# Differential attention scores: the high-part products of two maps moved into two 64-row halves of the array

## The chip, the cores and the metric

The kernel runs on one core of a Trainium2 chip. The metric is the device time of one execution in microseconds (us). Three runs of the kernel before are shown; beside them stands the profile of one execution. Names used below: PE is TensorE's matrix multiplication, PEld its weight load, DVE is VectorE, ACT is ScalarE, POOL is GpSimd, SP is the engine that issues most DMAs.

## The reference, cut to what matters

One decoder layer for 1024 tokens of width 1024: a projection `z = rms_norm(x) @ w_in`, then two branches side by side (differential softmax attention with 8 heads, gated linear attention with 4 heads), then an output projection with `w_out`, a norm and the residual. The change touches the attention scores alone:

```python
def diff_attention(q, k, v, lam):      # q, k: (B, S, 8 heads, 2 maps, 64)
    q = q * (DA_HEAD_DIM ** -0.5)
    s = jnp.einsum('bqhmd,bkhmd->bhmqk', qb, k)          # per block of 128 queries
    p = jax.nn.softmax(jnp.where(mask, s, -jnp.inf), axis=-1)
    w = p[:, :, 0] - lam * p[:, :, 1]                    # the two maps' difference
    return jnp.einsum('bhqk,bkhv->bqhv', w, v)
```

Each head has two maps, and the contraction of a score is over 64 numbers.

## The kernel before, in words

All products run in float32r. To keep accuracy, an operand is split in two: a high part (the value copied to float32r) and a low part (what is left), and a product `a*b` is built from products of the parts.

**Scores.** In `take` the projected q and k of a head are split and written to DRAM tiles `qk_d` of the shape [map, part, 64, 1024], part 0 being high and part 1 low. `load_qk` brings half a sequence (512 columns) back: the tile `q` holds, for each map, the high part on partitions 0 to 63 and the low part on 64 to 127; `k` holds the same order; `ks` holds k with the two parts swapped. For each block of 128 queries (`qb`, from 7 down to 0) and each map, `scores` multiplies q with k (high times high plus low times low, in one pass over all 128 rows) and q with ks (the two cross terms, in a second pass), both into one PSUM bank. A causal block of n = (qb+1)*128 keys is cut into parts of at most 512 columns (`parts_of`). There are three score banks, used in rotation (`sc_bank`). As each bank is done, DVE reads it with the mask and a running minimum (the instruction that writes `p`); after a map's last part ACT takes the exponential; after the second map DVE, POOL and DVE combine both maps to the weights. In the last head some narrow blocks are multiplied 512 wide, so that the bank is fully written.

**The work around it.** `merge` interleaves three generators into one program order for PE: `all_scores`, `all_values` (which transposes the weights in `turn`, splits them, and multiplies with v in `weigh`, 34 of merge's time units behind the scores) and `out_early` (the output projection's partial sums, tiles `ypart`). Each generator gives the merge an estimated cost at each yield, and the merge takes the one whose planned time is least. `scores` yields once after each DVE read of a bank, so that other PE work can be placed between the passes of one map and those of the next. PE keeps this program order (`mm` pins it); the other engines' order is planned by the framework. `load_qk` for the next head is called when block 4 of a head has been scored, and its DMAs go to SP's queue; `qk_load` remembers the last of them, behind which the gate and v loads are placed.

Every matrix multiplication of the kernel goes through line 142, so groups of instructions are told apart by their tiles: `sc` are the scores, `wtr` the transposed weights, `po` the weighted values, `ypart` and `yps` the output projection, `gkl_ps` a small projection to 64 output columns early in the kernel.

Of the kernel before, what the change touches and what calls it, by code (L numbers as in the profile page):

```python
# [9 lines left out]
F32R = mybir.dt.float32r  # L10
# [4 lines left out]
P = 128  # L15
# [5 lines left out]
DA_HEADS = 8  # L21
# [4 lines left out]
QA, KA, VA, GA, QB, KB, VB, GB, GKL = 0, 1024, 2048, 3072, 4096, 4608, 5120, 6144, 7168  # L26
# [5 lines left out]
def hymba_kernel(  # L32
# [21 lines left out]
    pe, sp = nc.tensor, nc.sync  # L54
# [22 lines left out]
    def fp(t):  # L77
        return t.bitcast(F32)

    def cols(half):  # L80
        return slice(half * 512, half * 512 + 512)
# [47 lines left out]
    def bank(i, shape, name):  # L129
        return psum.tile(shape, F32, tag=f"b{i}", name=name)  # L130
# [10 lines left out]
    def mm(*a, **k):  # L141
        tc.keep_in_program_order(pe.matmul(*a, **k))  # L142
# [32 lines left out]
    kp = ctx.enter_context(tc.tile_pool(name="kp", bufs=1))  # L175
# [9 lines left out]
    def t_st(name, dt=F32):  # L185
        return t2k("st", 4, name, dt)
# [73 lines left out]
    i = order.index((1, 4))  # L260
# [176 lines left out]
    def take(kind, n, half, unit, c):  # L437

        cs = cols(half)
        if kind in ("QA", "KA"):  # L440
            h = n + unit

            ending = made[0] > len(order) - LEAD
            if ending and order[made[0] - 1][1] == 7:
                raw = ap.tile([P, 2, 512], F32R, tag="raw", name="qk_st", bufs=4)
                hi, lo = raw[:, 0], raw[:, 1]
            else:
                hi, lo = t_st("qk_hi", F32R), c.bitcast(F32R)
            scale = -0.125 if kind == "QA" else 1.0
            act.activation(hi, c, AF.Copy, scale=scale)  # L450
            dve.scalar_tensor_tensor(lo, c, scale, fp(hi), ALU.mult, ALU.subtract)
            d = qk_d["q" if kind == "QA" else "k"][h]
            for t, src in enumerate((hi, lo)):
                for m in range(2):
                    ins = sp.dma_start(d[m, t, :, cs], fp(src)[64 * m : 64 * m + 64])
                    if ending:
                        tc.keep_in_program_order(ins)
        elif kind in ("GA", "GB"):
            g = t_st("g")
            act.activation(g, c, AF.Exp, scale=-1.0)  # L460
            act.activation(g, g, AF.Ln, bias=1.0)
            act.activation(g, g, AF.Exp, scale=-1.0)
            dve.tensor_tensor(c, c, g, ALU.mult)
            d = g_d[n + unit] if kind == "GA" else gg_d[n][unit]
            sp.dma_start(d[:, cs], c)
        elif kind == "QB":
            g = n + unit
            e_q, _ = decs[g]
            qd = t_st("gqd")
            dve.scalar_tensor_tensor(c, c, QSCALE, e_q[:, cs], ALU.mult, ALU.mult)  # L470
            dve.tensor_tensor(
                qd.rearrange("p (n i) -> p n i", i=P),
                c.rearrange("p (n i) -> p n i", i=P),
                dsteps[g][:, half * 4 : half * 4 + 4].unsqueeze(2).to_broadcast([P, 4, P]),
                ALU.mult,
            )
            for t, src in enumerate((c, qd)):
                sp.dma_start(gq_d[g][t, :, cs], src)
        else:
            g = n + unit  # L480
            dve.tensor_tensor(c, c, decs[g][1][:, cs], ALU.mult)
            sp.dma_start(gq_d[g][2, :, cs], c)
# [54 lines left out]
    def step(i):  # L537
# [25 lines left out]
        def done(half, unit, p0, p1):  # L563
            if wide(p):
                return take_values(p, half, unit, p0, p1)
            c = t_c("c")
            dve.tensor_tensor(c, p0, p1, ALU.add)
            take(kind, m, half, unit, c)
# [452 lines left out]

    def load_qk(h, n, half):

        if h % 2 and half == 0 and n != "q":
            t = smps[0].tile([P, 2, 512], F32R, tag=f"{n}0", name=f"{n}0")
        else:
            t = kp.tile([P, 2, 512], F32R, tag=f"{n}{half}", name=f"{n}{half}")
        for m in range(2):
            d = qk_d["q" if n == "q" else "k"][h][m, :, :, cols(half)]
            if n != "ks":  # L1030
                ins = sp.dma_start(fp(t[:, m]), d.rearrange("t p s -> (t p) s"))
            else:
                for i in range(2):
                    ins = sp.dma_start(fp(t[64 * i : 64 * i + 64, m]), d[1 - i])
        qk_load[:] = [ins.ins]
        qk[h, n, half] = t

    qk, smps, qk_load = {}, [], []
# [8 lines left out]
    for n in ("q", "k", "ks"):  # L1047
        load_qk(0, n, 1)
        if n != "q":
            load_qk(0, n, 0)  # L1050
# [87 lines left out]
    def parts_of(n):  # L1138
        return [(0, n)] if n <= 512 else [(0, 512), (512, n)]
# [15 lines left out]
    def sc_bank(name, shape):  # L1155
        n_sc[0] += 1
        return bank(SC[n_sc[0] % 3], shape, name)
# [8 lines left out]
    def scores(h, qb):  # L1166

        n = (qb + 1) * P
        qc = slice(qb % 4 * P, qb % 4 * P + P)
        st = const.tile([P, 6], F32, tag="stt", name="stt", bufs=4)  # L1170
        p0 = pp.tile([P, n], F32, tag=f"p0_{qb}", name="p0", bufs=1 + (qb > 5))
        p1 = smp.tile([P, S], F32, tag="p1", name="p1", bufs=2)
        for m, p in enumerate((p0, p1)):
            q = qk[h, "q", qb // 4][:, m, qc]
            parts = parts_of(n)
            if h == DA_HEADS - 1 and (qb, m) in ((1, 1), (0, 0), (0, 1)):

                parts = [(0, 512)]
            for i, (a, b) in enumerate(parts):
                sc = sc_bank("sc", [P, 512])  # L1180
                for j, name in enumerate(("k", "ks")):
                    for half in range(2):
                        lo, hi = max(a, half * 512), min(b, half * 512 + 512)
                        if lo < hi:
                            mm(
                                sc[:, lo - a : hi - a], q,
                                qk[h, name, half][:, m, lo - half * 512 : hi - half * 512],
                                start=(j == 0), stop=(j == 1),
                            )
                e = min(b, n)  # L1190
                last = i == len(parts) - 1

                behind = tc.issue_after(lowest[0]) if (h, qb) == (0, NT - 2) else nullcontext()
                with behind:
                    ins = dve.tensor_tensor_reduce(
                        p[:, a:e], sc[:, : e - a],
                        maskt[:, NZ + P - (e - a) :] if last else maskt[:, : e - a],
                        1.0, 3e38 if i == 0 else st[:, 4 + m : 5 + m], ALU.add, ALU.min,
                        st[:, m : m + 1] if last else st[:, 4 + m : 5 + m],
                    )  # L1200
                if (h, qb) == (0, NT - 1):
                    lowest[:] = [ins.ins]
                c = 0.08 + (e - a) / 512 * 0.56
                if last:
                    act.activation(
                        p[:, :n], p[:, :n], AF.Exp, bias=st[:, m : m + 1], scale=-1.0,
                        accum_out=st[:, 2 + m : 3 + m],
                    )
                if last and m:
                    dve.reciprocal(st[:, 4:6], st[:, 2:4])  # L1210
                    pool.tensor_scalar(
                        p1[:, :n], p1[:, :n], st[:, 5:6], lam, ALU.mult, ALU.mult
                    )
                    dve.scalar_tensor_tensor(
                        p0[:, :n], p0[:, :n], st[:, 4:5], p1[:, :n], ALU.mult, ALU.subtract
                    )
                    w[h, qb] = p0
                    c += 0.25 + n / 1024 * 1.4
                yield c
# [3 lines left out]
    def all_scores():  # L1223
        for h in range(DA_HEADS):
            for qb in range(NT - 1, -1, -1):
                if qb in (3, 5) and h:
                    yield lambda h=h, half=qb // 4: (h - 1, half) in used
                yield from scores(h, qb)
                if qb == 4 and h + 1 < DA_HEADS:
                    for n in ("q", "k", "ks"):  # L1230
                        load_qk(h + 1, n, 1)
                    for n in ("k", "ks"):
                        load_qk(h + 1, n, 0)
            if h + 1 < DA_HEADS:
                load_qk(h + 1, "q", 0)
        scored.append(True)
        opened.update(dict.fromkeys(SC))
# [444 lines left out]
```

## Time and profile before

| | |
|---|---|
| time, median of 3 runs | 973.4 us (973.16 to 973.76) |
| span of the profiled execution | 971.1 us; its page gives no other time of that execution |
| PE busy in the span | 958.7 us (99%), 4977 matmuls and as many weight loads |
| DVE, ACT, POOL busy in the span | 735.5 us (76%), 604.6 us (62%), 207.9 us (21%) |
| mean granted TensorE clock | 0.999 |
| first to last score matmul | 625.8 to 897.1 us of the span |

How to read it: a row of matmuls names the tiles (out<-in), the rows and columns of the array that it uses (128*128), the moving operand's shape (128x512), and its count. The "busy" of a group counts overlapping time once, and a matmul's duration runs to its modelled end, which lies after the start of the next one. What a matmul costs the stream is therefore read from the distance between starts, in the timeline, whose rows give the start, the duration and how many instructions a row holds.

### The profile page before, as it was taken

What the parts mean: (1) busy time and instruction counts of PE and PEld (TensorE: products, weight loads), DVE (VectorE), ACT (ScalarE), POOL (GpSimd) and SP (SyncE); (2) the same over time, 40 slices, a digit from 0 to 9 for tenths busy, and PEclk for the clock granted to TensorE, in tenths of its full rate; (3) what the DMA queues carried; (4) which work ended last, traced back from release to release, by engine and by line L of the source; (5) the groups of instructions that cost most, each with busy time, mean ns of one, the idle gap of its engine ahead of it and who ended that gap; (6) DMA issues with size and microseconds to landing.
All of it is one profiled execution on the core that took longest, in us unless ns stands there. A gap on an engine that the chain in (4) does not pass through costs nothing.

```text
span 971.1 us, 15096 instructions
## 1 busy us (share of the span) xinstructions
PE 958.7 (99%) x4977; PEld 814.5 (84%) x4977; DVE 735.5 (76%) x1464; ACT 604.6 (62%) x1166; POOL 207.9 (21%) x266
## 2 busy tenths in 40 slices
PE   8999999999999999999999999999999999999997
PEld 7998988888888888888888888878888888888786
DVE  5996698897687686686766576587888888898554
ACT  8752364764667555576665344366786787887773
POOL 4300001212141221231100002121322222443322
PEclk9999999999999999999999999999999999999999
DMA  9433366578568987986754588996656769994777
GB/s 347 163 103 117 101 192 225 170 239 294 199 210 255 300 272 251 302 277 212 259 177 152 163 251 269 401 336 203 221 170 218 241 200 355 334 286 106 152 210 148
DMA packets 151293, 220.39 MB, mean 227 GB/s; under 512 B 15728, under 2 KB 86384, under 8 KB 151120
## 3 DMA queue, kind: packets, MB, share of 16 engines
q1 hardware_dynamic: 137056, 178.70, 56.8%
q0 software_dynamic: 14160, 40.74, 14.5%
q8 instruction: 39, 0.64, 0.3%
q14 instruction: 38, 0.31, 0.1%
HBM read 133.93 MB, written 88.60 MB: 229 GB/s over the span
## 4 chain that ended last, share of the span: by engine, by line
PE 94%; ACT 3%; DVE 1%; issue 1%; DMA 0%; POOL 0%; DVEq 0%; ACTq 0%; POOLq 0%
PE x L142 23%; PE z L142 16%; PE y L142 16%; PE ypart L142 13%; PE sc L142 7%; PE po L142 5%; PE yps L142 4%; PE wtr L145 3%; PE gpo L142 3%; PE kv L142 1%; ACT junk L66 1%; PE gkl_ps L142 1%; PE pa L142 1%; DVE p L66 1%; ACT h_hi L66 0%
## 5 line engine op out<-in xcount | busy, mean ns | idle before, releaser
L66 ACT CAST w<-w_raw 128x512 fp32r<-128x512 f32 (+1 forms) x150 | 98.0, 655 | 92.3 <-PE y L142 46.4
L66 DVE TENSOR_TENSOR w<-w_raw,w 128x512 fp32r<-128x512 f32 (+1 forms) x150 | 109.3, 732 | 48.8 <-ACT w L66 44.6
L66 ACT ACTIVATE p<-p,stt 128x896 f32<-128x896 f32 (+7 forms) x128 | 99.3, 777 | 36.2 <-DVE stt L66 35.2
L66 ACT COPY s<-x 128x512 f32<-128x512 f32 x82 | 47.8, 586 | 88.8 <-PE x L142 88.2
L66 POOL TENSOR_SCALAR p<-p,stt,lam 128x1024 f32<-128x1024 f32 (+3 forms) x64 | 56.2, 879 | 147.7 <-DVE stt L66 143.8
L66 DVE CUSTOM_DVE_ANT_0 p<-sc,maskt 128x512 f32<-128x512 f32 (+3 forms) x128 | 74.3, 585 | 14.2 <-PE sc L142 12.9
L66 POOL DMA_DIRECT2D wo_d<-wo_hi x32 | 17.5, 545 | 313.9 <-ACT wo_hi L66 313.9
L142 PE MATMUL z<-s_hi,w 128*128 128x512 f32 x320 | 80.2, 393 | 0.0
L142 PE MATMUL x<-s_hi,w 128*128 128x512 f32 x320 | 80.1, 392 | 0.0
L142 PE MATMUL y<-h_hi,w 128*128 128x512 f32 x320 | 80.0, 392 | 0.0
L142 PE MATMUL ypart<-wo_hi,m_hi 128*128 128x512 f32 x192 | 79.5, 414 | 0.1
L142 PE MATMUL ypart<-wo_hi,m_lo 128*128 128x512 f32 x192 | 75.5, 393 | 0.0
L142 PE MATMUL ypart<-wo_lo,m_hi 128*128 128x512 f32 x192 | 75.4, 393 | 0.0
L142 PE MATMUL sc<-k,q 128*128 128x512 f32 (+1 forms) x192 | 69.1, 363 | 1.4 <-DVE stt L66 1.3
L142 PEld LDWEIGHTS z<-s_hi,w 128*128 128x128 f32 x320 | 59.7, 188 | 12.3
L142 PEld LDWEIGHTS y<-h_hi,w 128*128 128x128 f32 x320 | 59.7, 188 | 12.3
L142 PEld LDWEIGHTS x<-s_hi,w 128*128 128x128 f32 x320 | 59.7, 188 | 12.3
L66 DVE TENSOR_TENSOR w_raw<-w_raw 128x512 f32<-128x512 f32 (+1 forms) x88 | 66.1, 751 | 1.9 <-DMA w_raw<-in_w_in_dram 0.8
L142 PE MATMUL sc<-ks,q 128*128 128x512 f32 (+1 forms) x192 | 66.0, 347 | 0.0
L66 ACT CAST wt_hi<-wtr 128x512 fp32r<-128x512 f32 (+1 forms) x80 | 42.8, 535 | 25.1 <-PE wtr L145 24.3
L66 DVE TENSOR_TENSOR wt_lo<-wtr,wt_hi 128x512 fp32r<-128x512 f32 (+1 forms) x80 | 50.6, 633 | 8.9 <-ACT wt_hi L66 8.2
L66 DVE TENSOR_TENSOR c<-z,s 128x512 f32<-128x512 f32 x48 | 32.8, 688 | 30.6 <-ACT s L66 20.3
(225 smaller groups left out, 2351.7 us busy)
## 6 DMA issues: line engine op xcount, KB each, us to landing
w_raw<-in_w_in_dram SPq DMA_DIRECT2D x48, 512.0 KB, 4.9
wo_d<-wo_hi POOLq DMA_DIRECT2D x32, 256.0 KB, 3.8
q<-q_d SPq DMA_DIRECT2D x32, 256.0 KB, 4.7
k<-k_d SPq DMA_DIRECT2D x32, 256.0 KB, 5.5
ks<-k_d SPq DMA_DIRECT2D x64, 128.0 KB, 6.0
v<-v_d SPq DMA_DIRECT2D x16, 512.0 KB, 7.0
wo_raw<-in_w_out_dram POOLq DMA_DIRECT2D x31, 256.0 KB, 4.8
wo_d<-gqd POOLq DMA_DIRECT2D x22, 256.0 KB, 4.2
```

Of the source, the lines that this page charges most:

```text
L66: ins = op(*a, **k)
L142: tc.keep_in_program_order(pe.matmul(*a, **k))
L145: tc.keep_in_program_order(pe.transpose(dst, src, ident))
```

## The change

In the DRAM tiles the parts are put in another order, by map: q has [high; low] for map 0 and [low; high] for map 1; k has [low; high] for map 0 and [high; low] for map 1. A full load of k's tile now gives `ks`, with the parts opposite to q's. The tile `k` shrinks to [128, 512]: the high part of map 0 on partitions 0 to 63 and the high part of map 1 on partitions 64 to 127. `scores` takes both maps of a part together: it takes two score banks, issues the two cross passes (128 rows, q with ks), then the two products of the high parts (64 rows each, in rows 0 to 63 and in rows 64 to 127), and then the reads. The product of the two low parts is left out. The count of matmuls stays the same, and the yields to `merge` stay after each bank's read.

```diff
+                    at_t = t ^ m if kind == "QA" else 1 - (t ^ m)
+                    ins = sp.dma_start(d[m, at_t, :, cs], fp(src)[64 * m : 64 * m + 64])
...
+        shape = [P, 512] if n == "k" else [P, 2, 512]
...
-            if n != "ks":
+            if n != "k":
                 ins = sp.dma_start(fp(t[:, m]), d.rearrange("t p s -> (t p) s"))
             else:
-                for i in range(2):
-                    ins = sp.dma_start(fp(t[64 * i : 64 * i + 64, m]), d[1 - i])
+                ins = sp.dma_start(fp(t[64 * m : 64 * m + 64]), d[1 - m])
...
-        for m, p in enumerate((p0, p1)):
-            q = qk[h, "q", qb // 4][:, m, qc]
...
-                sc = sc_bank("sc", [P, 512])
-                for j, name in enumerate(("k", "ks")):
-                    for half in range(2):
...
+        for i, (a, b) in enumerate(parts):
+            half, last, e = a // 512, i == len(parts) - 1, b
+            widths = [b - a] * 2
+            if h == DA_HEADS - 1 and qb < 2:
+
+                widths = [b - a if qb else 512, 512]
+            scs = [sc_bank("sc", [P, 512]) for _ in range(2)]
+            for m, sc in enumerate(scs):
+                mm(
+                    sc[:, : widths[m]], q[:, m, qc], qk[h, "ks", half][:, m, : widths[m]],
+                    start=True, stop=False,
+                )
+            for m, sc in enumerate(scs):
+                rows = slice(64 * m, 64 * m + 64)
+                mm(
+                    sc[:, : widths[m]], q[rows, m, qc], qk[h, "k", half][rows, : widths[m]],
+                    start=False, stop=True,
+                )
+            for m, (p, sc) in enumerate(zip((p0, p1), scs)):
```

More of the change, by code (lines that the diff above doesn't have):

```diff
@@ L454, in take @@
                 for m in range(2):
-                    ins = sp.dma_start(d[m, t, :, cs], fp(src)[64 * m : 64 * m + 64])
+                    at_t = t ^ m if kind == "QA" else 1 - (t ^ m)
+                    ins = sp.dma_start(d[m, at_t, :, cs], fp(src)[64 * m : 64 * m + 64])
                     if ending:
@@ L1022, in load_qk @@
     def load_qk(h, n, half):
+        shape = [P, 512] if n == "k" else [P, 2, 512]
         if h % 2 and half == 0 and n != "q":
-            t = smps[0].tile([P, 2, 512], F32R, tag=f"{n}0", name=f"{n}0")
+            t = smps[0].tile(shape, F32R, tag=f"{n}0", name=f"{n}0")
         else:
-            t = kp.tile([P, 2, 512], F32R, tag=f"{n}{half}", name=f"{n}{half}")
+            t = kp.tile(shape, F32R, tag=f"{n}{half}", name=f"{n}{half}")
         for m in range(2):
             d = qk_d["q" if n == "q" else "k"][h][m, :, :, cols(half)]
-            if n != "ks":
+            if n != "k":
                 ins = sp.dma_start(fp(t[:, m]), d.rearrange("t p s -> (t p) s"))
             else:
-                for i in range(2):
-                    ins = sp.dma_start(fp(t[64 * i : 64 * i + 64, m]), d[1 - i])
+                ins = sp.dma_start(fp(t[64 * m : 64 * m + 64]), d[1 - m])
         qk_load[:] = [ins.ins]
@@ L1172, in scores @@
         p1 = smp.tile([P, S], F32, tag="p1", name="p1", bufs=2)
-        for m, p in enumerate((p0, p1)):
-            q = qk[h, "q", qb // 4][:, m, qc]
[L1175 to L1179, printed above, removed]
-                sc = sc_bank("sc", [P, 512])
-                for j, name in enumerate(("k", "ks")):
-                    for half in range(2):
[L1183 to L1191, printed above, removed]
+        q = qk[h, "q", qb // 4]
+        parts = parts_of(n)
+        for i, (a, b) in enumerate(parts):
[16 more added lines that the diff above has]
+            for m, (p, sc) in enumerate(zip((p0, p1), scs)):
                 behind = tc.issue_after(lowest[0]) if (h, qb) == (0, NT - 2) else nullcontext()
```

## The prediction

> **What bounds the kernel now.** I read the page first: the span, each engine's busy time, and the chain of work that ended last.
>
> ```profile
> span 971.1 us, 15096 instructions
> PE 958.7 (99%) x4977; PEld 814.5 (84%) x4977; DVE 735.5 (76%) x1464; ACT 604.6 (62%) x1166; POOL 207.9 (21%) x266
> ...
> PE 94%; ACT 3%; DVE 1%; issue 1%; DMA 0%; POOL 0%; DVEq 0%; ACTq 0%; POOLq 0%
> PE x L142 23%; PE z L142 16%; PE y L142 16%; PE ypart L142 13%; PE sc L142 7%; PE po L142 5%; PE yps L142 4%; PE wtr L145 3%; PE gpo L142 3%; PE kv L142 1%; ACT junk L66 1%; PE gkl_ps L142 1%; PE pa L142 1%; DVE p L66 1%; ACT h_hi L66 0%
> ```
>
> PE is the bound, and the scores are 7% of the chain. Next the stretches: the stage with the scores and what follows it.
>
> ```profile
> 625.00:898.00 273.00, 271.22 (x1435) 229.69 (x1436) 228.91 (x628) 200.92 (x440) 79.70 (x86) 1.00 0.76 245
> 898.00:971.00 73.00, 66.27 (x310) 54.21 (x308) 38.99 (x92) 45.54 (x114) 18.23 (x20) 0.98 0.72 169
> ```
>
> The columns after the length are PE, PEld, DVE, ACT and POOL busy, the granted clock and DMA. In the stage PE is busy for 271.2 of 273 us, and DVE, the next, for 228.9 (84%). The waits of PE in that stage are two lines:
>
> ```profile
> PE sc L142 <- DVE stt L66: 1.3, 2, 1.1
> PE wtr L145 <- DVE p L66: 0.4, 1, 0.4
> ```
>
> So a PE microsecond saved here is a microsecond of the kernel, as long as nothing else becomes late; no DMA stands among these waits.
>
> **What a matmul costs the stream.** The score tile's own instructions:
>
> ```profile
> L142 PEld LDWEIGHTS sc<-k,q x192: 186/188/192, 625.6 to 896.7; 128*128 128x128 f32 x192
> L142 PE MATMUL sc<-k,q x192: 218/389/504, 625.8 to 896.8; 128*128 128x512 f32 x99, 128*128 128x384 f32 x32, 128*128 128x256 f32 x31, 128*128 128x128 f32 x30
> L142 PE MATMUL sc<-ks,q x192: 273/387/398, 626.0 to 897.1; 128*128 128x512 f32 x99, 128*128 128x384 f32 x32, 128*128 128x256 f32 x31, 128*128 128x128 f32 x30
> ```
>
> A 512-wide pass has a modelled length of 389 ns, but the stream pays the distance between starts, from the timeline:
>
> ```profile
> 73.29 1.12 PE L142 MATMUL x<-w,s_lo 128*128 128x256 f32 x8
> 74.24 2.00 PE L142 MATMUL gkl_ps<-h_hi,wl 128*64 128x512 f32 x8
> 76.08 2.00 PE L142 MATMUL gkl_ps<-h_lo,wl 128*64 128x512 f32 x8
> 77.91 2.08 PE L142 MATMUL z<-w,s_hi 128*128 128x256 f32 x16
> 79.83 1.12 PE L142 MATMUL z<-w,s_lo 128*128 128x256 f32 x8
> ```
> ```profile
> 405.15 0.39 PE L142 MATMUL gpo<-gqd,gu 128*128 128x128 f32 x2
> ...
> 406.94 0.39 PE L142 MATMUL gpo<-gqd,gu 128*128 128x128 f32 x2
> ```
> ```profile
> 705.04 0.52 PE L142 MATMUL po<-wt_hi,v 128*128 128x384 f32 x2
> 705.40 0.33 PE L142 MATMUL po<-wt_lo,v 128*128 128x384 f32 x1
> 705.57 0.39 PE L142 MATMUL ypart<-wo_hi,m_hi 128*128 128x512 f32 x1
> ```
>
> 512 columns: (77.91-76.08)/8 = 0.229 us. 384: (705.57-705.04)/3 = 0.177. 256: (79.83-77.91)/16 = 0.120. 128: eight rows of two from 405.15 to 406.94, 1.79/16 = 0.112. The last does not halve with the width: there the weight load sets the pace. That agrees with the durations of weight loads, 188 ns for 128 columns against 134 for 64:
>
> ```profile
> L142 PEld LDWEIGHTS gkl_ps<-h_hi,wl x12: 133/134/138, 74.1 to 82.2; 128*64 128x64 f32 x12
> ```
>
> 64 columns take 54 ns more, so 128 take about 108, and a load is hidden behind the matmul before it unless that one is narrow.
>
> The k passes thus cost 99 x 0.229 + 32 x 0.177 + 31 x 0.120 + 30 x 0.112 = 35.4 us, and so do the ks passes: 70.8 us of the 971.
>
> **The change on PE.** The ks passes stay (35.4 us). The 192 k passes become 96 pairs of half-row passes: 50 with 512 columns (two of them from the widened blocks of the last head, one of these with 256 beside 512), 16 with 384, 15 with 256, 15 with 128. If the two of a pair stream at the same time they cost 50 x 0.229 + 16 x 0.177 + 15 x 0.120 + 15 x 0.112 = 17.8 us, a saving of 17.7. Weight loads do not shrink: there are still four per pair, each of 128 columns, and four need 4 x 0.112 = 0.448 us. With 256 columns three passes take 0.360 and with 128 columns 0.336, so the loads take over: 15 x 0.088 + 15 x 0.112 = 3.0 us back. Saving 14.7 us. No row shows two passes streaming side by side or a pass of 64 rows, so this is bounded: from 17.7 us (loads of the two halves also run together) to nothing (the halves run one after the other). I take 14.7: the rows above show that the columns streamed and the load set the pace, and the halves share neither rows nor bank. The Trainium skill, "TensorE: Matmul & The Clock Gate", section "Part 3: Packing small matmuls", says that tiles in different row groups start about 4 ns apart; by that the side-by-side case holds, and no run shown here tests it.
>
> A term inside this: the second half's weight load. In the stream a load begins as the matmul before it starts. If the load of half B waits for half A to start, B starts 0.112 us after A, and a pair of halves costs 0.112 more where it was not already load-bound: 50 x 0.112 for 512 columns, and for 384 columns 16 x 0.112; in the narrow ones it is inside the 0.448. The saving is then 14.7 - 7.4 = 7.3 us. I take the hidden load, since the halves load different rows, and keep 7.3 for a rival.
>
> A second term is the switch between 128 rows and 64 rows, twice per pair, 192 times. The nearest rows are those of `gkl_ps`, which runs on 128*64: the stream goes from 128*128 to 128*64 at 74.24 and back at 77.91. The eight 256-wide passes before it take (74.24-73.29)/8 = 0.119 each, the switch included, and the eight before 77.91 take 0.229 like any other. A switch of columns costs nothing that shows, so I take 0 for a switch of rows. The upper bound is that a switch waits until the pass before has left the array: 389 - 229 = 160 ns, and another 188 ns if the weights load only after that.
>
> **The change on the banks.** A pair needs two of the three banks at once. Before, a bank came back after three units of map and part (3 x 273/192 = 4.27 us on average); now the second bank of a pair is the first one of the pair before, 2 x 273/192 = 2.84 us. What stands against PE is how late DVE reads:
>
> ```profile
> L66 DVE CUSTOM_DVE_ANT_0 p<-sc,maskt 128x512 f32<-128x512 f32 (+3 forms) x128 | 74.3, 585 | 14.2 <-PE sc L142 12.9
> DVE p L66 <- PE sc L142: 16.2, 29, 1.3
> ```
>
> In 29 of 192 reads DVE waited for the bank; in the others it came later. I went through the timeline for the 95 places where a pair follows a pair, comparing the end of DVE's first read with the start of the next pair's first pass plus 0.229. In 11 places the bank would come too late, by 3.9 us together. The first and the last of them:
>
> ```profile
> 630.38 0.39 PE L142 MATMUL sc<-k,q 128*128 128x512 f32 x1
> ...
> 631.03 0.69 DVE L66 CUSTOM_DVE_ANT_0 p<-sc,maskt 128x512 f32<-128x512 f32 x1 [0.45 <-PE sc L142]
> 631.18 0.40 PE L142 MATMUL sc<-k,q 128*128 128x512 f32 x1
> ```
> ```profile
> 841.79 0.48 PE L142 MATMUL sc<-k,q 128*128 128x512 f32 x1
> ...
> 842.57 0.40 PE L142 MATMUL sc<-k,q 128*128 128x512 f32 x1
> ```
> ```profile
> 842.53 0.69 DVE L66 CUSTOM_DVE_ANT_0 p<-sc,maskt 128x512 f32<-128x512 f32 x1 [1.31 <-PE sc L142]
> ```
>
> These are places where the merge put several score units in a row. The first bank's data now also come one cross pass later (0.229 us), which makes 11 x 0.229 = 2.5 us more: 6.4 at the outside by this count, and up to 9 if a stream that is 5% faster meets more late reads. Against it, the second map's data are ready together with the first's, which takes some of DVE's 16.2 us of waiting away, and a stall lets DVE catch up. I take 5 us, between 0 and 9. Behind a stalled score pass everything on PE waits, `po`, `wtr` and `ypart` included, since PE keeps the program order.
>
> **What else moves.** The writes only go to other addresses. Of the loads
>
> ```profile
> k<-k_d SPq DMA_DIRECT2D x32, 256.0 KB, 5.5
> ks<-k_d SPq DMA_DIRECT2D x64, 128.0 KB, 6.0
> ```
>
> `k` halves and `ks` goes from 64 to 32 DMAs of twice the size: 32 issues and 4 MB fewer on SP's queue, the loads of `v` and `gate` behind them a little earlier. PE waits for no DMA in the stage, so I cost this at nothing. If that cover went, it could only gain. The exponentials of the two maps now follow each other more closely on ACT, which is 200.9 of 273 us busy; the transposes that need them come many units later, so nothing here either. DVE is not the floor yet: if only its waits for scores vanished, the stage would still last 273 - 16.2 = 256.8 us, and I ask for 263.3.
>
> **The sum**, against the profiled span: 971.1 - 14.7 + 5 = 961.4 us. The runs' median of 973.4 is 2.3 above that span; I keep these 2.3 as they lie outside it: 963.7 us.
>
> **The rivals.**
>
> *The switch drains the array (slower).* Each of the 192 switches costs 160 ns, with the next weights already loaded: 192 x 0.160 = 30.7 us. 973.4 - 14.7 + 30.7 = 989.4, with a little bank stall left at most, since pairs come slower: 990. With weights loaded only after the drain it is 192 x 0.348 = 66.8, and 1025 us. It decides from (14.7 - 5)/192 = 50 ns per switch. For it speaks that the modelled end of a pass lies 160 ns after the next start, so passes overlap in the array, and a changed geometry may forbid that. Against it speak the two switches of columns that cost nothing. The Trainium skill has this as a rule ("TensorEngine Tiling (Array Packing)", section "Tiling Modes"): changing the tiling mode, not only the tile, drains TensorE. On the change to 128*64 this case's trace does not agree (0.119 us per pass, switch included); rows are not shown.
>
> *The drain is partial.* At 30 to 70 ns a switch, 6 to 13 us, the gain of 9.7 is about gone: 970 to 977, around 973.
>
> *The second half's load is exposed.* 973.4 - 7.3 + 4 = 970.1 us (fewer stalls, since pairs are longer). The rows speak for it in that every load starts with the matmul before it; against it, that A and B fill different rows.
>
> *The halves do not run side by side.* Then there are four passes as before, no gain, and the bank stalls: 973.4 + 0 + 4 = 977.4. The change would not do what it says. Nothing in the trace tests it.
>
> **How the numbers follow.** Forecast 0.42, exposed load 0.15, partial drain 0.07, halves in turn 0.08, full drain 0.22, drain with load 0.06. The predicted time is the forecast's, 963.7 us; its own range goes from 973.4 - 17.7 = 955.7 (no stalls, loads together) to 973.4 - 14.7 + 9 = 967.7. The range for 8 in 10 reaches over the rivals up to the drain at 990: 956 to 992, leaving out the drain with load and the best end. Three runs before span 0.6 us, so 0.2% (1.9 us) is about what can be told from no change. Faster: 0.42, of the exposed load 0.13, of the partial drain 0.01, together 0.56. Slower: both drains 0.28, halves in turn 0.07, partial 0.02, together 0.37. The same: 0.07.
>
> **What the profile after would show.** Rows of `sc<-k,q` on 64*128, 192 of them, and 192 of `sc<-ks,q` on 128*128. Right: in the timeline two half passes with almost the same start, the next full pass 0.23 us after them, and the pass before them at 0.23 too; stage from 625 about 10 us shorter. Drain: 0.35 us or more between the start of the second cross pass and the first half, and again after the pair. Exposed load: 0.11 between the halves. In turn: 0.23 between them. Banks: PE waiting for `stt` or `p` of DVE before `sc`, about 5 us in place of 1.3. What would make me wrong beyond these: PE waits for DVE of tens of us, which would mean that the pairing, not the array, decides.

## The result and the profile after

The changed kernel takes 1005.0 us (median of 4 runs, 1004.6 to 1005.7) against 973.35: ratio 1.0327, 95% interval [1.0312, 1.0342]. It is 31.7 us slower; 963.7 was forecast.

The page of the changed kernel, its lines on the span, the engines' busy time and the chain by engine:

```profile
span 1004.0 us, 15084 instructions
PE 981.4 (98%) x4977; PEld 799.4 (80%) x4977; DVE 737.0 (73%) x1464; ACT 602.9 (60%) x1166; POOL 203.6 (20%) x266
...
PE 90%; DVE 3%; DMA 2%; issue 1%; SPq 1%; ACT 1%; POOL 1%; DVEq 0%; POOLq 0%; ACTq 0%
```

The work of DVE, ACT and POOL is what it was. PE has 22.7 us more of busy time and 10 us more without any. The stage with the scores (PE, PEld, DVE, ACT, POOL busy after the length):

```profile
625.00:930.00 305.00, 292.83 (x1433) 213.58 (x1431) 228.66 (x626) 197.97 (x436) 78.92 (x85) 0.99 0.66 209
```

It lasts some 32 us longer than the 273 before, and the profiled spans differ by 32.9, so nearly the whole loss is here. PE's waits in it, with total, times and longest:

```profile
PE ms L142 <- DVE sq_hl L66: 7.7, 6, 2.7
PE sc L142 <- DVE stt L66: 4.4, 5, 1.7
```

Before, PE's waits in the stage were 1.7 us, and none of them was for `ms`. The score passes themselves:

```profile
L142 PEld LDWEIGHTS sc<-k,q x192: 182/183/286, 626.8 to 928.7; 64*128 64x128 f32 x192
L142 PE MATMUL sc<-k,q x192: 322/491/580, 626.8 to 928.7; 64*128 64x512 f32 x99, 64*128 64x384 f32 x32, 64*128 64x256 f32 x31, 64*128 64x128 f32 x30
```

The passes have 64 rows, as intended, and a median length of 491 ns where the full ones had 389. One pair of 384 columns in PE's timeline (start, length, count in the row), then the weight loads of the same place:

```profile
701.73 0.51 PE L142 MATMUL sc<-ks,q 128*128 128x384 f32 x2
702.17 0.44 PE L142 MATMUL sc<-k,q 64*128 64x384 f32 x2
702.54 0.50 PE L142 MATMUL ypart<-wo_hi,m_hi 128*128 128x512 f32 x1
702.88 0.39 PE L142 MATMUL ypart<-wo_hi,m_lo 128*128 128x512 f32 x1
703.11 0.40 PE L142 MATMUL ypart<-wo_lo,m_hi 128*128 128x512 f32 x1
```
```profile
701.51 0.41 PEld L142 LDWEIGHTS sc<-ks,q 128*128 128x128 f32 x2
702.17 0.18 PEld L142 LDWEIGHTS sc<-k,q 64*128 64x128 f32 x2 [0.25 <-issue]
```

Both halves stand in one row that is 0.44 us long, where 32 such passes have a mean length of 0.437 each: they run side by side, and so do their weight loads. But three distances are too long. The two cross passes take 0.44 up to the halves where 0.354 is usual (+0.09). From the halves to the next full pass it is 0.37, where a single 384-wide pass takes 0.177 (+0.19). And the first full pass after them keeps the stream for 0.34 instead of 0.229 (+0.11). Together 0.39 us per pair. The weight loads show one reason: those of the cross passes begin at 701.51, as the pass before them starts, but those of the halves begin only at 702.17, with the halves. With 512 columns, at 706.64, the last two distances read +0.20 and +0.11, and the first full pass after the halves, too, has its weights loaded only as it starts (707.06):

```profile
706.64 0.49 PE L142 MATMUL sc<-k,q 64*128 64x512 f32 x2
707.07 0.50 PE L142 MATMUL ypart<-wo_hi,m_hi 128*128 128x512 f32 x1
707.41 0.40 PE L142 MATMUL ypart<-wo_hi,m_lo 128*128 128x512 f32 x1
```
```profile
706.64 0.18 PEld L142 LDWEIGHTS sc<-k,q 64*128 64x128 f32 x2 [0.37 <-issue]
707.06 0.19 PEld L142 LDWEIGHTS ypart<-wo_hi,m_hi 128*128 128x128 f32 x1 [0.24 <-issue]
```

So a switch of rows costs about 0.2 us. I read it as some 0.09 until the array is empty and some 0.1 of a weight load that nothing hides. The late loads are in the timeline; that the 0.09 is the emptying is not shown (by the modelled ends, the second cross pass lasts until 702.24, past the start of the halves). 96 x 0.39 = 37.4 us stand against the 17.7 saved. That explains 20 of the 33 us; the rest has to be looked for in waits.

### The profile page after: what moved, and what is told of

It is laid out like the page before. It is cut to its first block, busy times and chain, and to the rows that moved or that the text cites. A ratio compares the mean times of both kernels' runs of the same rounds, so it can differ in the third digit from the quotient of the medians.

```text
span 1004.0 us, 15084 instructions
## 1 busy us (share of the span) xinstructions
PE 981.4 (98%) x4977; PEld 799.4 (80%) x4977; DVE 737.0 (73%) x1464; ACT 602.9 (60%) x1166; POOL 203.6 (20%) x266
## 4 chain that ended last, share of the span: by engine, by line
PE 90%; DVE 3%; DMA 2%; issue 1%; SPq 1%; ACT 1%; POOL 1%; DVEq 0%; POOLq 0%; ACTq 0%
PE x L142 22%; PE z L142 15%; PE y L142 15%; PE ypart L142 13%; PE sc L142 7%; PE po L142 5%; PE yps L142 4%; PE wtr L145 3%; PE gpo L142 3%; PE kv L142 1%; DMA w_early<-in_w_in_dram 1%; DVE p L66 1%; PE gkl_ps L142 1%; PE pa L142 1%; PE ms L142 1%
## 5 line engine op out<-in xcount | busy, mean ns | idle before, releaser
L66 DVE CUSTOM_DVE_ANT_0 p<-sc,maskt 128x512 f32<-128x512 f32 (+3 forms) x128 | 72.1, 584 | 25.6 <-PE sc L142 24.9
L142 PE MATMUL ypart<-wo_hi,m_hi 128*128 128x512 f32 x192 | 86.3, 450 | 0.1
L142 PE MATMUL sc<-ks,q 128*128 128x512 f32 (+1 forms) x192 | 54.3, 359 | 4.4 <-DVE stt L66 4.4
L66 DVE SCALAR_TENSOR_TENSOR p<-p,stt,p 128x1024 f32<-128x1024 f32 (+3 forms) x64 | 52.1, 814 | 8.6 <-POOL p L66 8.1
L66 DVE TENSOR_TENSOR c<-z,s 128x512 f32<-128x512 f32 x48 | 32.9, 688 | 31.6 <-ACT s L66 19.9
```

The costliest lines, as they stand in the source:

```text
L66: ins = op(*a, **k)
```

## The experiments

Theories at the start: SWITCH (0.2 us for each change between 128 and 64 rows), PAIRING (the new order, with two banks at a time, holds the loss) and PASS (a 64-row pass is dear wherever it stands).

**e1_pairs_full: the order alone.**

```diff
-                    sc[:, : widths[m]], q[rows, m, qc], qk[h, "k", half][rows, : widths[m]],
+                    sc[:, : widths[m]], q[:, m, qc], qk[h, "k", half][:, m, : widths[m]],
```
(with the loads and the DRAM order of the kernel before)

> Loads, DRAM order and all four products as in the kernel before; of the change only the order: both maps of a part in two banks at once, cross passes first, then the k passes, all on 128 rows. Theory SWITCH (each change between 128 and 64 rows costs about 0.196 us, 0.391 us per pair, 37.6 us in all, against 17.7 us saved): no switch here, so 973 to 979 us, what is over 973.4 being stalls on banks and late DVE work. Rival PAIRING (the array gains its 17.7 us, the pair order costs 49): 1022 us. Rival PASS (a 64-row pass is dear in itself, whatever stands beside it): 973 to 979 us, as SWITCH.

989.3 us, ratio 1.0165 [1.0148, 1.0182]. None had it: half of the loss, 16 us, is there without a single 64-row pass, and the array's part is the other half, 15.7. By the two traces DVE runs its instructions in nearly the same order in both (11 of 1464 places differ), so the 15.7 can be put down to the passes. PE's waits:

```profile
PE ms L142 <- DVE sq_hl L66: 7.5, 6, 2.6
PE sc L142 <- DVE stt L66: 5.1, 6, 1.7
```

They are nearly those of the changed kernel. They sum to 12.6 us, against 1.7 before. The other 5.2 us of the loss count as busy time of PE (963.9 us against 958.7): a wait shows as idle only from the modelled end of the pass before, 0.16 us after the next start is due, so short waits are not seen. What makes up the 5.2 us was not followed. PAIRING is right as to its existence and wrong in its size; SWITCH needs a second cause beside it.

**e2_four_switches: the same passes, map by map.**

```diff
             for m, sc in enumerate(scs):
                 mm(sc..., q[:, m, qc], qk[h, "ks", half]..., start=True, stop=False)
-            for m, sc in enumerate(scs):
                 rows = slice(64 * m, 64 * m + 64)
                 mm(sc..., q[rows, m, qc], qk[h, "k", half][rows...], start=False, stop=True)
```

> The changed kernel with the four passes of a pair in another order: cross pass of map 0, half pass of map 0, cross pass of map 1, half pass of map 1. Four switches per pair instead of two, and the halves no longer side by side. SWITCH: 1005.0 + 192 x 0.196 (37.6) + 17.7 = 1060 us, 1050 to 1062 with some stalls hidden by the slower PE. PASS (the price hangs on the count of 64-row passes, which is the same) and PAIRING: 1005.0 + 17.7 = 1023 us.

1043.7 us, ratio 1.0724 [1.0708, 1.0740]: 38.7 more than the changed kernel, where a price per pass allows 17.7. PASS falls. It is less than the 55 of SWITCH; the wait for `ms` shrinks to 1.6 us with the slower PE and none for `sc` is left, which accounts for some 10 us of it. Here the planner also put DVE's work in another order (some 200 of 1464 places differ); e14 gives the comparison without that.

**e3_columns: a switch of columns in the same places.**

```diff
-                    sc[:, : widths[m]], q[rows, m, qc], qk[h, "k", half][rows, : widths[m]],
+                    sc[:64, : widths[m]], q[:, m, qc][:, :64], qk[h, "k", half][:, m, : widths[m]],
```

> As e1_pairs_full, but the k passes run on 128 rows and 64 columns: only 64 of each block's 128 queries get this term, the other 64 are left out. The array's geometry changes at the same places as in the changed kernel, in columns instead of rows, and the two passes stand one after the other. If only a switch of rows drains: the time of e1_pairs_full, 973 to 979 us. If any switch of geometry drains: 973.4 + 37.6 = 1011 us or a little more.

990.1 us, ratio 1.0174 [1.0158, 1.0189], the time of e1. Its timeline:

```profile
701.53 0.71 PE L142 MATMUL sc<-ks,q 128*128 128x512 f32 x2
702.08 0.62 PE L142 MATMUL sc<-k,q 128*64 128x512 f32 x2
702.54 0.39 PE L142 MATMUL ypart<-wo_hi,m_hi 128*128 128x512 f32 x1
702.77 0.40 PE L142 MATMUL ypart<-wo_hi,m_lo 128*128 128x512 f32 x1
```

Two passes on 128*64 take 0.46 us, then 0.23 as always. The 0.55 of the two cross passes ahead of them is no switch: e1, all on 128*128, has it in the same place (701.15 to 701.70). Here columns switch for nothing; rows do not.

**e4_single_half: no pairing, four switches.** The loop of the kernel before, one map and one bank at a time, with the changed data:

```diff
+                mm(sc[:, : b - a], q, qk[h, "ks", half][:, m, : b - a], start=True, stop=False)
+                mm(sc[:, : b - a], q[rows], qk[h, "k", half][rows, : b - a], start=False, stop=True)
```

> The changed kernel's data and tiles, but the order of the kernel before: one map and one bank at a time, a cross pass on 128 rows, then its high parts on 64 rows. No pairing, four switches per two maps, no halves side by side. SWITCH: 973.4 + 384 x 0.196 (75.2) = 1049 us, 1045 to 1055. PAIRING: 973 to 976 us. PASS (0.196 us per 64-row pass): 973.4 + 37.6 = 1011 us.

1041.3 us, ratio 1.0698 [1.0682, 1.0714]. 68.0 us for 384 switches, with nothing side by side, no wait of PE in the stage, and DVE's order that of the kernel before but for 7 of 1464 places: 0.177 us per switch, the cleanest price. 192 x 0.177 - 17.7 = 16.3, near the 15.7 between e1 and the changed kernel.

**e5_same_rows: the halves one after the other.**

```diff
-                rows = slice(64 * m, 64 * m + 64)
+                rows = slice(0, 64)
```

> The changed kernel with both half passes of a pair on rows 0 to 63; map 1 thus gets the wrong operands for this term (its low parts of q with map 0's high parts of k), the work has the same shape. The switches stay two per pair. If the two halves really stream side by side in the changed kernel, that is lost here: 1005.0 + 17.7 = 1022.7 us, 1017 to 1023 with some stalls hidden by the slower PE. If they gained nothing: 1005 us.

1018.7 us, ratio 1.0469 [1.0454, 1.0485]: 13.7 more than the changed kernel.

```profile
700.86 0.73 PE L142 MATMUL sc<-k,q 64*128 64x512 f32 x2
701.52 0.50 PE L142 MATMUL ypart<-wo_hi,m_hi 128*128 128x512 f32 x1
```

The pair takes 0.66 here and 0.43 in the changed kernel, so running side by side does save one pass, 0.23 us. All engines run in the order of the changed kernel. The rest of the 17.7 is hidden because PE's waits fall by 4.0 us: for `sc` from 4.4 to 1.8, for `ms` from 7.7 to 6.3.

**e6_rows_only: all score passes on 64 rows.** DRAM order as before the change; k loaded once, with both parts.

```diff
+            for tq, tk in ((0, 0), (0, 1), (1, 0)):
+                for m, sc in enumerate(scs):
+                    rows = slice(64 * m, 64 * m + 64)
+                    mm(sc[:, : widths[m]], q[rows, tq, qc], qk[h, "k", half][rows, tk, : widths[m]], ...)
```

> The scores wholly in 64-row passes: per pair three side-by-side pairs of halves (high x high, high x low, low x high; map 0 in rows 0 to 63, map 1 in rows 64 to 127), k loaded once with both parts, no swapped copy. Still two switches per pair, but the halves now also follow other halves. If the price (drain and bare weight load) falls only at a change of rows: as the changed kernel, 1000 to 1007 us. If every 64-row pass pays for its own weight load of about 0.108 us because loads are not hidden in this geometry: 1005 + 2 x 96 x 0.108 (20.7) = 1026 us.

1006.3 us, ratio 1.0350 [1.0326, 1.0374], as the changed kernel.

```profile
702.32 0.40 PE L142 MATMUL ypart<-wo_lo,m_hi 128*128 128x512 f32 x1
702.64 0.96 PE L142 MATMUL sc<-k,q 64*128 64x512 f32 x6
703.54 0.50 PE L142 MATMUL ypart<-wo_hi,m_hi 128*128 128x512 f32 x1
703.87 0.39 PE L142 MATMUL ypart<-wo_hi,m_lo 128*128 128x512 f32 x1
```

Before the six passes +0.09 (0.32 for 0.229), after them +0.10 (0.33), and 0.90 for three rounds that need 0.69: +0.21, which I read as the bare load on the way in and the emptying on the way out. 0.40 in all, as for a single round of halves. The price falls on the change, not on the pass.

**The second cause: e7 and e8.** In e1 and in the changed kernel PE waits longest for `ms`, the norm's matmul. The place at 857 us of the changed kernel, DVE's timeline and then PE's:

```profile
856.80 0.69 DVE L66 CUSTOM_DVE_ANT_0 p<-sc,maskt 128x512 f32<-128x512 f32 x1 [0.53 <-PE sc L142]
...
857.41 0.69 DVE L66 CUSTOM_DVE_ANT_0 p<-sc,maskt 128x512 f32<-128x512 f32 x1
...
858.03 0.69 DVE L66 TENSOR_TENSOR m_lo<-m_raw,m_hi 128x512 fp32r<-128x512 f32 x1
858.63 1.28 DVE L66 SCALAR_TENSOR_TENSOR p<-p,stt,p 128x1024 f32<-128x1024 f32 x1
859.94 0.69 DVE L66 TENSOR_TENSOR sq_hl<-sq,sq_hl 64x512 fp32r<-64x512 f32 x1
```
```profile
857.67 0.40 PE L142 MATMUL ypart<-wo_lo,m_hi 128*128 128x512 f32 x1
860.77 0.47 PE L142 MATMUL ms<-sq_hl,ones 128*128 128x512 f32 x1 [2.71 <-DVE sq_hl L66]
```

`sq_hl` stands in DVE's queue behind both reads of a pair and more, and PE stands still. The same place in the kernel before, on DVE, where `sq_hl` comes ahead of the reads and PE does not wait:

```profile
833.68 0.69 DVE L66 TENSOR_TENSOR wt_lo<-wtr,wt_hi 128x512 fp32r<-128x512 f32 x1 [0.31 <-ACT wt_hi L66]
834.40 0.88 DVE L66 TENSOR_TENSOR sq_hl<-sq,sq_hl 64x512 fp32r<-64x512 f32 x1
835.31 0.69 DVE L66 CUSTOM_DVE_ANT_0 p<-sc,maskt 128x512 f32<-128x512 f32 x1
```

It is so in all six places where e1 waits for `ms`: between the steps that make `sq` and `sq_hl`, DVE's order has both reads of a pair, and in the kernel before one or none. Two runs put `ms` later in PE's order:

```diff
-        for _ in range(4):
+        for _ in range(6 if h < DA_HEADS - 1 else 4):
             yield 0.0
```

> e1_pairs_full with the norm's matmul (ms) placed two yields, one unit of the value stream, later in PE's order, for all heads but the last. In e1_pairs_full the passes before ms lost 8.5 us in six places, waiting for DVE's sq_hl. If that wait is a matter of order: 989.3 - 8.5 = 981 us, the rest above 973.4 being the waits for score banks. If DVE is late as a whole, the stall comes back before the next score, transpose or value pass: 985 to 990 us.

> The changed kernel with the same later ms. There the passes before ms lost 8.7 us. If a matter of order: 1005.0 - 8.7 = 996 us; if DVE is late as a whole: 1000 to 1005 us. Either way slower than 973.4, since the switches are untouched.

e7: 986.5 us, ratio 1.0139 [1.0122, 1.0156]. e8: 1003.3, ratio 1.0320 [1.0294, 1.0346]. They gain 2.8 and 1.7 us, not 8.5, and the runs of e8 lie between 1002.1 and 1007.8, so that its 1.7 can't be told from nothing. In e7 the wait for `ms` falls to 2.7 us and that for `sc` rises:

```profile
PE sc L142 <- DVE stt L66: 7.1, 8, 2.0
...
PE ms L142 <- DVE sq_hl L66: 2.7, 3, 1.1
```

The place of `ms` alone is not the cause; most of the wait goes elsewhere.

**e9, e10, e11: the end of a block issued later.** One guess was that DVE's reciprocal, waiting for two bunched exponentials, keeps the next reads back.

```diff
+                if i == 0 and m and todo:
+                    todo.pop()()
                 if last and m:
-                    dve.reciprocal(st[:, 4:6], st[:, 2:4])
...
+                    todo.append(combine)     # reciprocal, scaling and combination
```

> e1_pairs_full with the end of each block (reciprocal, POOL's scaling, DVE's combination of the two maps) issued after the reads of the next block's first pair. Theory TAIL: in the pair order the exponentials of both maps come together, DVE's reciprocal waits for ACT (17.8 us instead of 12.0), and the next reads stand behind it in DVE's queue, so banks come free late; moved back, most of the 16 us go: 973 to 980 us. Rival BANKS: two of three banks at once are too few whatever DVE's order: 985 to 989 us.

> The changed kernel with the same later end of each block. TAIL: only the array's price is left, 973.4 + 37.6 - 17.7 = 993 us, 989 to 995. BANKS: 1001 to 1005 us.

> The kernel before with the same later end of each block, as a control: PE waits only 1.7 us in the score stage there, so 972 to 974 us by both theories.

990.0 (1.0173 [1.0158, 1.0188]), 1005.5 (1.0332 [1.0317, 1.0348]) and 974.0 us (1.0008 [0.9998, 1.0017]). The control stays at no change, and the other two tell nothing: in e9 PE, DVE, ACT and POOL run their instructions in exactly the order of e1, as the planner places them by its own times and not by the order of issue. The same holds of e10 and the changed kernel.

**e12 and e15: the same, forced.** The end's DVE instructions are queued behind the second read of the next block's first pair.

```diff
                 if i == 0 and m and todo:
-                    todo.pop()()
+                    with tc.issue_after(ins.ins):
+                        todo.pop()()
```

> e9 left every engine's order as it was: the planner places the tail by its own times. Here the tail's DVE instructions are forced behind the reads of the next block's first pair; 110 places of DVE's order change against e1_pairs_full. TAIL (DVE's reads stand behind a reciprocal that waits for two exponentials): most of the 16 us go, 973 to 980 us. BANKS (a pair holds two of three banks, whatever DVE's order): 985 to 990 us.

> The changed kernel with the forced tail of e12. TAIL: only the array's price is left, 989 to 995 us. BANKS: 1000 to 1006 us.

e12: 989.2 us, ratio 1.0168 [1.0153, 1.0183]; e15: 1005.9, ratio 1.0339 [1.0322, 1.0356]. The times of the kernels that they were made from. The waits of e12:

```profile
PE wtr L145 <- DVE p L66: 6.1, 7, 1.3
PE ms L142 <- DVE sq_hl L66: 4.5, 7, 1.0
PE sc L142 <- DVE stt L66: 2.9, 5, 0.7
```

The waits for banks did shrink (5.1 to 2.9), but now the transposes wait for the weights that this tail makes. Moving DVE's work about does not give the time back; by itself this run does not say what the first cause is.

**e13_two_banks: the kernel before with less slack.**

```diff
-        return bank(SC[n_sc[0] % 3], shape, name)
+        return bank(SC[n_sc[0] % 2], shape, name)
```

> The kernel before, its order untouched, with its score units rotating over two banks instead of three. Every unit then gets its bank back after two units, as the second unit of every pair does in the pair order. BANKS: 985 us or more. TAIL: the exponentials are not bunched here, 974 to 979 us.

987.7 us, ratio 1.0156 [1.0141, 1.0171]. With the old order and nothing paired, one bank less costs 14.9 us, near the 16 of the pair order:

```profile
PE sc L142 <- DVE stt L66: 8.4, 15, 1.1
PE wtr L145 <- DVE p L66: 1.2, 2, 0.8
```

But the waits lie elsewhere: all but 1.2 us at score passes, and none before `ms`. The planner also gave DVE another order than in the kernel before (some 200 of 1464 places). The run shows that fewer free banks cost that much; that it is the same loss as in e1 it does not show, and that the sums are so near may be chance.

**e14_pairs_by_map: pairs, but one bank finished early.**

```diff
             for m, sc in enumerate(scs):
                 mm(sc..., q[:, m, qc], qk[h, "ks", half]..., start=True, stop=False)
-            for m, sc in enumerate(scs):
                 mm(sc..., q[:, m, qc], qk[h, "k", half]..., start=False, stop=True)
```

> e1_pairs_full with the four passes of a pair in the order map 0 cross, map 0 k, map 1 cross, map 1 k: the first bank is complete one pass (0.23 us) earlier and the second is needed one pass later (0.23 us). BANKS: in some 20 tight places 0.46 us each come back, 989.3 - 9 = 980 us, 978 to 985. TAIL: the reads are late for DVE's own reasons, 986 to 990 us.

978.7 us, ratio 1.0059 [1.0044, 1.0074]: 10.6 of the 16 us come back with another order of the four passes.

```profile
PE ms L142 <- DVE sq_hl L66: 2.7, 3, 1.3
PE sc L142 <- DVE stt L66: 1.1, 3, 0.6
```

Both waits fall, the one for `ms` too, which this edit doesn't touch directly. The order of the four passes, with what the planner makes of it, holds two thirds of the loss. Whether the banks' slack or DVE's order gives it back stays open, since the edit also changes the planner's order on DVE (some 200 of 1464 places). For `ms` the order on DVE goes with it: of the six places, three (at 732, 805 and 840 us) now have one read of a pair ahead of `sq_hl` instead of two, and there the waits, 0.84, 1.45 and 2.65 us in e1, are 0.01. e14 is also e2 with all passes on 128 rows, with nearly the same order on DVE (13 places): e2 takes 65.0 us more for 384 switches, 0.169 each, beside the 0.177 of e4. This order finishes map 0 before map 1 is begun, so it can't be had with the halves side by side; with halves in it (e2) there are four switches.

No version here beats the kernel before.

## Why the prediction was wrong, point by point

- **The bound and where the loss falls: right.** PE bounds the stage, and all of the change in time lies in it.
- **The cost of a pass and the saving of 17.7 us: right in kind.** e5 shows one pass saved per pair. The weight loads of the two halves run together, so the 3.0 us that I took off for narrow blocks, and the rival with the second half's load exposed, were not needed: both loads stand in one row of 0.18 us.
- **The switch: the step that failed.** A switch of rows is a term that I took as 0, from the switch between 128*128 and 128*64, and gave the drain 0.28. e3 confirms the column switch at zero in the very same places, and e4 gives a switch of rows 0.177 us: the nearest row was of another kind. The rival had the mechanism, with 0.160 if weights were loaded already and 0.348 if not. What is seen looks like a part of each: 0.09 before the halves, read as emptying, and about 0.1 of bare load. 192 x 0.177 is 34.0 us, twice the 17.7 saved. The Trainium skill's rule ("TensorEngine Tiling (Array Packing)", section "Tiling Modes"), that changing the tiling mode drains TensorE, fits the price of rows here and not the columns of e3. The figure of the Trainium skill in "TensorE: Matmul & The Clock Gate", section "Part 3: Packing small matmuls", about 4 ns between tiles of different rows, agrees with the one row of 0.44 us that both halves share, at 0.437 us for each.
- **The banks: the second step that failed, a term too small.** I took 5 us, with 9 as the upper bound; the order costs 16.0 (e1). The waits for banks came out as taken, 5.1 us in e1, with some luck: I had counted 11 short ones, and there are 6, of up to 1.7 us. What I left out is what else on PE waits for DVE: 7.5 us before `ms`, where DVE's new order puts both reads of a pair ahead of `sq_hl`, and 5.2 us more that the page counts as PE's busy time, whose cause was not followed. My count took DVE's timeline as it stood before, so it could not show that.
- **The drain rival at 990** went without the bank stalls, as I expected a slower PE to hide them. It does so with four switches (e2), not with two: 4.4 and 7.7 us of waits remain. 989.3 of the order alone and 15.7 of the array make the 1005.0. Term by term: -17.7 for the pass, +34.0 for the switches and +16.0 for the order come to +32.3, and +31.7 was measured; I had -14.7, 0 and +5.
- **The signs named for the profile** told it: 0.35 us or more between the second cross pass and the first half was the mark of a drain, and it reads 0.27 with 384 columns (0.44 for both cross passes, less 0.177), 0.09 above the usual distance: I had set that mark too high, and the marks after the pair (0.37 and 0.34) show the other part. Of waits for DVE in tens of us, the mark for a pairing that decides, 12.1 us came: the pairing is half of the loss, and the array the other half.

## What to carry to other kernels

Halving the contraction of a product pays only if the stream stays on those rows: by these figures, 0.177 us per change and 0.229 us per pass saved, a pair of changes must cover at least two saved 512-wide passes, or neighbouring work must be on 64 rows too. Before a change takes two units of a rotating buffer at once, try the old order with one buffer less: it costs one line, and here it would have warned of a loss of 14.9 us where the order cost 16.0, though its waits lay in other places. And price a wait not by the instruction that waits alone, but by all that the late engine feeds, in the order that the planner will give it.

## What the runs showed of the hardware

- Two 64-row passes in different rows start together (one row of 0.44 us for both, 384 columns), and their weight loads do too (one row of 0.18 us).
- A change between 128 and 64 rows costs 0.177 us in this stream, the mean over both ways (e4). The weights of the first pass after a change are loaded only as it starts (702.17, 707.06), where a load in this stream otherwise begins with the pass before. Three rounds of 64-row passes pay the 0.40 us per pair no more often than one round does (e6).
- A change between 128 and 64 columns costs nothing that can be read (e3: two passes in 0.46 us).
